# Sums of x in tiles of their own, no GpSimd work in the feed-forward stages until the norm, bias tables as tasks of the schedule

## The chip, the cores and the metric

The kernel runs on one core of one Trainium2 chip. The core has five engines with an instruction queue each, worked through in order: TensorE (PE, matmuls; its loads of weights are listed as PEld), VectorE (DVE), ScalarE (ACT), GpSimd (POOL) and SyncE (SP, which here issues most DMA transfers). Matmul results lie in eight banks of PSUM, named b0 to b7. An instruction that waits for another engine or for a transfer holds up all that is queued behind it on its engine. The metric is the device time of one execution in microseconds.

## The reference, cut

One layer of an encoder over 1024 prompt and 64 sample positions (1088 columns), width 1024, feed-forward width 2816, all in float32:

```python
def _swiglu(x, wi, wo):
    a, u = jnp.split(x @ wi, 2, axis=-1)
    return (jax.nn.silu(a) * u) @ wo

h = LN1(alpha*x + 0.5*SwiGLU1(x))
z = h @ w_in                        # all projections and gates
o_a = sparse attention (index, top 256 keys, T5 bias)
o_b = band attention (own chunk + 8 before, relative bias)
m = (sigmoid(g_a)*(o_a@w_branch_a) + sigmoid(g_b)*(o_b@w_branch_b)) @ w_out
h = LN2(alpha*h + m)
y = LN3(alpha*h + 0.5*SwiGLU2(h))
```

## The kernel before

**Precision.** A float32 product is made as three matmuls of a rounded type: each operand is split into a high part (a rounded copy) and a low part (the operand less its high part). A split so costs a copy ("hi") on ACT or DVE and a subtraction ("lo") on DVE or POOL. `factor` makes the split of a piece of the activations, `parts` inside `prepare` that of a 512-column piece of weights, in tiles w_s, of which there are two pairs (w_s0, w_s1).

**Stages.** The first feed-forward (0 to about 755 us), projections, attention and branches (to about 1760 us), the second feed-forward (to the end). Each feed-forward has a first stage (x @ wi, silu, product; about 500 us), a second stage of 63 items (h @ wo, about 200 us) and its last outputs with a layer norm. Nearly every traced instruction carries line 120 (L120), the helper `Timed.call` that records operations, so places in the program are named here by tiles.

**First stage.** The columns of the hidden layer are taken in 22 tiles f. From f=2 on, a tile's four block products are made by the scheme with seven products, in the order P2, P1, P6, P5, P3, P7, P4, of 48 matmuls each, with x cut in four blocks (two halves of rows, two of columns): A11, A12, A21, A22. P2 takes A12, P1 A11, P6 the sum S2 = S1 - A11, P5 S1 = A21 + A22, P3 S4 = A12 - S2 and P7 S3 = A11 - A21. `combos` makes these four sums from x (tiles y0 to y7, 128x544 halves), once, before and during f=2, one k of four at a time: sum on DVE or POOL, hi on ACT or DVE, lo on DVE or POOL, into tiles S1 to S4. The sums S1, S2, S4 are made in the tiles c1 and c2, S3 (`third`) in c0. c0, c1 and c2 (`G.t`) are also what every product uses: ACT copies the first product of a block from its banks (`c<-b`), which frees the banks for the next product, DVE adds the later ones to it (`c<-c,b`), silu and product run there, and 18 of the hidden tiles go from c by DMA to a buffer in DRAM (`ff_d<-c`).

**Second stage.** Each item is a product of 24 matmuls (about 3.0 us) of a factor of the kept hidden tiles with a sum of pieces of wo. The seven factors are again P2, P1, P6, P5, P3, P7, P4, nine items each: tiles a12, a11, a21, a22 are read from DRAM (`a<-ff_d`); sums of them (`a<-a,a`) are split into five tiles fac (`fac<-a`, `fac<-a,fac`). After a group of nine items DVE adds the eight banks to y (`y<-y,b`, eight instructions), and the next group's matmuls need those banks. The sums of pieces of wo were made during the first stage in tiles st (`sums_of_weights`, four sums per f on DVE from f=4 on: `st<-st,st`, loaded by `st<-in_wo_dram`) and put in DRAM.

**What sets the order.** A planner, class `Plan`, keeps queues of tasks and emulated clocks; it gives the next instruction to the queue whose turn its costs say it is. A task that may run on several engines (`shared`, `adders`, `w_h`, `x_h`) goes to the one that the emulated clocks say is free first, unless `st["solo"]` is true: then sums and lo parts go to DVE alone, hi parts to ACT alone. `solo` is set at the start of each feed-forward and cleared after seven of its steps (`SOLO`). The tables of bias for the attention (`bias_tables`: a load, a small matmul against `flip` or `btab` into bank 7, a copy on DVE, a store `bt_d<-one`, 16 times, DMAs on ACT's queue) run beside the first stage, stepped by a fixed rate of 0.3 steps per three matmuls.

Of the kernel before, what the change touches and what calls it, by code (L numbers as in the profile page):

```python
# [23 lines left out]
F32 = mybir.dt.float32  # L24
# [8 lines left out]
P = 128  # L33
# [297 lines left out]
def tile_trunk(ctx, tc, a):  # L331
# [520 lines left out]
    def combos(G, k):  # L852


        a11, a21, a12, a22 = (G.y[k + x][:, h * HT:(h + 1) * HT] for x in (0, 4) for h in range(2))
        s3, s1, s2 = (G.t[i].rearrange("p s c -> p (s c)") for i in range(3))

        def make(out, x, y, op, deps, reads):
            t = plan.task(shared(HT), "x_m", lambda e: of(e).tensor_tensor(out, x, y, op=op), deps, 2, None, reads)
            for i in (k, k + 4):  # L860
                G.read[i].append(t)
            return t

        def use(i, tasks):
            for s in range(2):
                G.user[i, s] = tasks

        def sums():
            m1 = make(s1, a21, a22, OP.add, G.used(1), [a21, a22])
            m2 = make(s2, s1, a11, OP.subtract, [m1] + G.used(2), [a11])  # L870
            t2 = factor(G, "S2", k, s2, [m2])
            m4 = make(s2, a12, s2, OP.subtract, [t2], [a12])
            use(1, [factor(G, "S1", k, s1, [m1]), m2])
            use(2, [factor(G, "S4", k, s2, [m4])])

        def third():
            m3 = make(s3, a11, a21, OP.subtract, G.used(0), [])
            use(0, [factor(G, "S3", k, s3, [m3])])
        return sums, third

    def add_ffn7(wi, wo, wl, G, gi, put, beside_it, last, end):
# [93 lines left out]
        def some():  # L975
            while G.hold and at.next < len(units):
                prepare()
# [202 lines left out]
        def sums_of_weights(j):  # L1180

            r = G.stage[j % 2]
            for i in range(4):
# [86 lines left out]
        def last_outputs():  # L1270
            fs = list(range(NF - 4, NF))
            wait(*(F[f].t[x, s] for f in fs for x in ("h1", "h2") for s in range(2)))
            last()
            some()
            us = [get_unit(f"l{d}", NF) for d in range(KT)]
# [89 lines left out]

        def normal():
            st["solo"] = False
        for i, j in enumerate(steps):
            if i == SOLO:
                jobs.append(normal)  # L1370
            jobs.append(j)
        jobs.append(last_outputs)
        jobs.append(end)

    HT, SUB = NT // 2, NT // 4
    EIGHT, SOLO = 2, 7
    SECONDS = (EIGHT + 1, NF - 1)
# [19 lines left out]
    def common(G):  # L1397
        G.xc, G.ready, G.user, G.read = {}, {}, {}, {d: [] for d in range(KT)}
        G.used = lambda i, s=None: [t for x in ((0, 1) if s is None else (s,)) for t in G.user.get((i, x), ())]
# [26 lines left out]
    def stage_tiles(G, name, side):  # L1426
        p = pool(open_(name), name, side)
        G.stage = [[p.tile([P, 512], F32, name=f"st{x}{i}") for i in range(4)] for x in range(2)]
        return p
# [13 lines left out]
    def make_ring1():  # L1443
        finish_streams()
        ring_tile(G1, "top1", None)
# [26 lines left out]
    def bias_tables():  # L1472


        one = G1.one
        row = one[:HEADS, :384]
        nc.scalar.dma_start(flip, a["flip"])
        yield
        for i in range(2):
            p = bank("ln")  # L1480
            kk = [(0, 32)] if i == 0 else [(0, 128), (128, 64)]
            for x, (k0, kn) in enumerate(kk):
                o = one[:, :384]
                nc.scalar.dma_start(o[:kn], a["hot_" + "ab"[i]][k0:k0 + kn])
                t = btab[:, x]
                nc.scalar.dma_start(t[:kn], a[("t5T", "relT")[i]][k0:k0 + kn])
                for _ in range(8):
                    yield
                nc.tensor.matmul(p[:HEADS, :384], t[:kn], o[:kn], start=x == 0, stop=x == len(kk) - 1)
                yield  # L1490
            nc.scalar.activation(row, p[:HEADS, :384], AF.Copy)
            for _ in range(2):
                yield
            nc.scalar.dma_start(row_d[i], row)
            for _ in range(8):
                yield
            for h in range(HEADS):
                t = one[:, :256]
                nc.scalar.dma_start(t, bass.AP(tensor=row_d[i].tensor, offset=row_d[i].offset + h * 384,
                                               ap=[[1, P], [1, 256]]))  # L1500
                for _ in range(8):
                    yield
                p = bank("ln")
                nc.tensor.matmul(p[:, :256], flip, t, start=True, stop=True)
                b = one[:, 256:]
                yield
                nc.vector.tensor_copy(b, p[:, :256])
                if i == 1:
                    nc.vector.tensor_scalar(b[:64, 192:], p[:64, 192:256], NEG, None, op0=OP.add)
                yield  # L1510
                nc.scalar.dma_start(bt_d[i][:, h * 256:(h + 1) * 256], b)
                yield

    def start_bias():
        beside(bias_tables(), 0.3)

# [1119 lines left out]
```

## Time and profile before

| | us |
|---|---|
| median of three runs | 2534.99 (2533.91 to 2536.92) |
| the profiled execution | 2534.35 |
| its span | 2532.5 |
| PE busy in it | 2438.6 (96%) |
| DVE, ACT, POOL busy | 1797.7 (71%), 1231.5 (49%), 477.1 (19%) |

The profile is one execution. A row of a timeline gives the start, the length in us, the engine, the tiles written and read, how many instructions are joined in the row, and in brackets how long the engine stood idle before it and what released it. The time of PE's instructions is modelled, so a stretch of the span is best weighed by how many matmuls it holds. PEclk is the mean granted clock of TensorE in a stretch, 1.00 being 2.4 GHz. In the view by stretches two columns follow it, the mean busy share of the DMA engines and what they moved in GB/s.

### The profile page before, as it was taken

To read this page: it belongs to the slowest core of one execution; us is meant where nothing else is said; L and a number is where in the kernel's file an instruction comes from. 1 tells how busy PE (TensorE), PEld (TensorE's weight loads), DVE (VectorE), ACT (ScalarE), POOL (GpSimd) and SP (SyncE) were. 2 spreads that over 40 slices of the span, in tenths; PEclk is the share of its full clock that TensorE was granted. 3 is DMA by queue.
4 is the path that set the end of the run, shared out by engine and by line. 5 is a ranking of instruction groups with operands and counts; after the bars stand their busy time and mean duration, and the time that the engine had idled before them with its cause. 6 is when DMAs were issued, how large, how long until landed. Compare 5 with 4: busy or idle time off the path is not lost.

```text
span 2532.5 us, 46846 instructions
## 1 busy us (share of the span) xinstructions
PE 2438.6 (96%) x17338; PEld 2382.9 (94%) x17338; DVE 1797.7 (71%) x4263; ACT 1231.5 (49%) x2611; POOL 477.1 (19%) x561
## 2 busy tenths in 40 slices
PE   9999999999999999999999999999989999999996
PEld 8999999999998899999999998998989999999995
DVE  6666655677776889898766767658866665668868
ACT  5333333322234598777857777524533333332224
POOL 0000000033233222122243332314000000003504
PEclk9999999999999999999999999999999999999997
DMA  5466533263222322322221112643246652245222
GB/s 182 120 191 195 174 103 90 78 202 112 84 81 94 117 75 77 96 81 82 71 79 59 56 39 69 191 145 116 77 126 191 192 156 90 64 138 189 84 72 71
DMA packets 221205, 285.42 MB, mean 113 GB/s; under 512 B 20704, under 2 KB 146512, under 8 KB 220944
## 3 DMA queue, kind: packets, MB, share of 16 engines
q1 hardware_dynamic: 200864, 257.40, 33.4%
q10 hardware_dynamic: 19552, 22.81, 2.8%
q8 instruction: 136, 2.23, 0.4%
q0 software_dynamic: 560, 2.21, 0.2%
q14 instruction: 93, 0.76, 0.1%
HBM read 207.62 MB, written 75.00 MB: 112 GB/s over the span
## 4 chain that ended last, share of the span: by engine, by line
PE 71%; DVE 11%; ACT 9%; issue 3%; DMA 3%; POOL 1%; ACTq 1%; SPq 0%; DVEq 0%; POOLq 0%
PE b L120 71%; ACT w L120 3%; ACT scores L120 2%; DVE w_s L120 2%; DVE y L120 1%; DVE w L120 1%; DVE k L120 1%; ACT pt L120 1%; DVE c L120 1%; DMA st<-in_wo_dram 1%; DVE pt L120 1%; ACT z L120 1%; DMA a<-ff_d 1%; DMA ff_d<-c 1%; ACTq L120 1%
## 5 line engine op out<-in xcount | busy, mean ns | idle before, releaser
L120 PE MATMUL b<-x,w_s 128*128 128x384 f32 (+1 forms) x3528 | 637.3, 332 | 4.7 <-ACT z L120 1.8
L120 PE MATMUL b<-A,w_s 128*128 128x272 f32 (+1 forms) x4824 | 633.9, 291 | 7.8 <-DVE y L120 3.4
L120 PEld LDWEIGHTS b<-A,w_s 128*128 128x128 f32 x4824 | 620.9, 190 | 12.1 <-ACT A L120 2.6
L120 PEld LDWEIGHTS b<-x,w_s 128*128 128x128 f32 x3528 | 587.5, 189 | 13.8 <-DVE x L120 2.4
L120 PE MATMUL b<-S,w_s 128*128 128x272 f32 x4032 | 520.4, 289 | 18.2 <-ACT c L120 18.2
L120 PEld LDWEIGHTS b<-S,w_s 128*128 128x128 f32 x4032 | 511.5, 189 | 22.2 <-ACT c L120 20.4
L120 ACT ACTIVATE w_s<-wr 128x512 fp32r<-128x512 f32 (+1 forms) x270 | 181.1, 671 | 368.5 <-PE b L120 223.1
L120 DVE TENSOR_TENSOR w_s<-wr,w_s 128x512 fp32r<-128x512 f32 (+1 forms) x323 | 247.4, 768 | 151.6 <-ACT w_s L120 142.3
L120 PE MATMUL b<-fac,w_s 128*128 128x272 f32 x1800 | 231.4, 290 | 4.4 <-DVE y L120 4.4
L120 PEld LDWEIGHTS b<-fac,w_s 128*128 128x128 f32 x1800 | 229.8, 190 | 4.9 <-issue 2.6
L120 POOL TENSOR_TENSOR w_s<-wr,w_s 128x256 fp32r<-128x256 f32 x196 | 149.8, 789 | 415.4 <-ACT w_s L120 169.9
L120 POOL TENSOR_TENSOR h<-c,h 128x272 fp32r<-128x272 f32 x2 | 1.5, 773 | 902.7 <-DVE h L120 902.7
L120 ACT ACTIVATE c<-b 128x272 f32<-128x272 f32 (+1 forms) x262 | 101.7, 391 | 104.7 <-PE b L120 90.2
L120 DVE TENSOR_TENSOR c<-c,b 128x272 f32<-128x272 f32 x240 | 103.5, 434 | 58.4 <-PE b L120 55.3
L120 DVE TENSOR_TENSOR pt<-b,pt 128x512 fp32r<-128x512 f32 (+4 forms) x184 | 96.5, 545 | 31.2 <-ACT pt L120 29.5
L120 ACT ACTIVATE fac<-a 128x544 fp32r<-128x544 f32 x75 | 49.4, 658 | 142.0 <-PE b L120 121.4
L120 PE MATMUL b<-pt,v 128*128 128x256 f32 (+3 forms) x672 | 103.6, 281 | 4.9 <-DVE pt L120 2.3
L120 PEld LDWEIGHTS b<-pt,v 128*128 128x128 f32 (+1 forms) x672 | 93.5, 188 | 13.6 <-DVE pt L120 4.5
L120 ACT ACTIVATE c<-c 128x272 f32<-128x272 f32 x160 | 68.7, 431 | 76.7 <-DVE c L120 73.8
L120 ACT ACTIVATE w<-w,mx 128x640 f32<-128x640 f32 (+5 forms) x144 | 100.5, 698 | 10.4 <-DVE mx L120 7.5
L120 ACT ACTIVATE w<-w,sm 128x640 f32<-128x640 f32 (+5 forms) x144 | 97.7, 697 | 9.7 <-DVE sm L120 4.6
L120 PE MATMUL b<-m,w_s 128*128 128x384 f32 (+1 forms) x576 | 99.7, 332 | 2.5 <-DVE w_s L120 1.4
(277 smaller groups left out, 3363.4 us busy)
## 6 DMA issues: line engine op xcount, KB each, us to landing
wr<-in_wi_dram SPq DMA_DIRECT2D x156, 256.0 KB, 3.1
ff_d<-c SPq DMA_DIRECT2D x144, 136.0 KB, 3.0
a<-ff_d SPq DMA_DIRECT2D x72, 272.0 KB, 3.7
st<-in_wo_dram SPq DMA_DIRECT2D x72, 256.0 KB, 5.3
tw_d<-st SPq DMA_DIRECT2D x72, 256.0 KB, 2.5
wr<-in_wz_dram SPq DMA_DIRECT2D x35, 512.0 KB, 3.7
wr<-tw_d SPq DMA_DIRECT2D x48, 256.0 KB, 2.7
q<-in_wi_dram SPq DMA_DIRECT2D x39, 256.0 KB, 3.1
```

The source lines that it names most:

```text
L120: r = real(*args, **kw)
```

## The change

Three edits. (1) `combos` makes the sums in the four tiles `G.stage[0]` (st00 to st03, now 544 wide; S1 in st0[k mod 2], S2 and S4 in st0[2 + k mod 2], S3 in st0[k mod 4]); who used one last is kept in `G.last`. The tiles c0, c1, c2 are no longer touched by it. (2) `solo` stays true through both stages and is cleared in `last_outputs`: until then all sums and lo parts go to DVE, all hi parts to ACT. That takes 41 POOL instructions from each feed-forward to DVE (30 `a<-a,a`, 11 lo parts) and, in each second stage, 47 hi copies of weights from DVE to ACT. (3) `bias_tables` yields an engine and an earliest time to the planner (`plan.chain`) instead of being stepped; `make_ring1` runs the planner until that chain is empty. Its last matmul stands at PE's instruction 3039 instead of 2970; the order of the other matmuls is the same.

```diff
@@ -853,7 +853,7 @@
         a11, a21, a12, a22 = (G.y[k + x][:, h * HT:(h + 1) * HT] for x in (0, 4) for h in range(2))
-        s3, s1, s2 = (G.t[i].rearrange("p s c -> p (s c)") for i in range(3))
+        s1, s2, s3 = (G.stage[0][i] for i in (k % 2, 2 + k % 2, k % 4))
         def make(out, x, y, op, deps, reads):
             t = plan.task(shared(HT), "x_m", lambda e: of(e).tensor_tensor(out, x, y, op=op), deps, 2, None, reads)
@@ -861,21 +861,20 @@
                 G.read[i].append(t)
             return t
-        def use(i, tasks):
-            for s in range(2):
-                G.user[i, s] = tasks
+        def last(x):
+            return G.last.get(x.tensor.name, [])
         def sums():
-            m1 = make(s1, a21, a22, OP.add, G.used(1), [a21, a22])
-            m2 = make(s2, s1, a11, OP.subtract, [m1] + G.used(2), [a11])
+            m1 = make(s1, a21, a22, OP.add, last(s1), [a21, a22])
+            m2 = make(s2, s1, a11, OP.subtract, [m1] + last(s2), [a11])
             t2 = factor(G, "S2", k, s2, [m2])
             m4 = make(s2, a12, s2, OP.subtract, [t2], [a12])
-            use(1, [factor(G, "S1", k, s1, [m1]), m2])
-            use(2, [factor(G, "S4", k, s2, [m4])])
+            G.last[s1.tensor.name] = [factor(G, "S1", k, s1, [m1]), m2]
+            G.last[s2.tensor.name] = [factor(G, "S4", k, s2, [m4])]
         def third():
-            m3 = make(s3, a11, a21, OP.subtract, G.used(0), [])
-            use(0, [factor(G, "S3", k, s3, [m3])])
+            m3 = make(s3, a11, a21, OP.subtract, last(s3), [])
+            G.last[s3.tensor.name] = [factor(G, "S3", k, s3, [m3])]
         return sums, third
     def add_ffn7(wi, wo, wl, G, gi, put, beside_it, last, end):
@@ -1179,7 +1178,7 @@
         def sums_of_weights(j):
-            r = G.stage[j % 2]
+            r = [x[:, :512] for x in G.stage[j % 2]]
             for i in range(4):
                 nc.sync.dma_start(r[i].rearrange("p (d c) -> p d c", d=4),
                                   wog[:, i % 2 * 4:i % 2 * 4 + 4, (2 * j + i // 2) * P:(2 * j + i // 2 + 1) * P])
@@ -1271,6 +1270,7 @@
             fs = list(range(NF - 4, NF))
             wait(*(F[f].t[x, s] for f in fs for x in ("h1", "h2") for s in range(2)))
             last()
+            st["solo"] = False
             some()
             us = [get_unit(f"l{d}", NF) for d in range(KT)]
             for b in range(3):
@@ -1363,17 +1363,12 @@
             want.append(((f"l{d}", NF), lambda q: q, wl[d // 2][:, d % 2 * 512:(d % 2 + 1) * 512]))
             unit(f"l{d}", NF)
-        def normal():
-            st["solo"] = False
-        for i, j in enumerate(steps):
-            if i == SOLO:
-                jobs.append(normal)
-            jobs.append(j)
+        jobs.extend(steps)
         jobs.append(last_outputs)
         jobs.append(end)
     HT, SUB = NT // 2, NT // 4
-    EIGHT, SOLO = 2, 7
+    EIGHT = 2
     SECONDS = (EIGHT + 1, NF - 1)
     SECOND, PAIRS = ("P2", "P1", "P6", "P5", "P3", "P7", "P4"), KEPT_OUT // 2
     NEEDS = dict(P2=("12",), P1=("11",), P6=("11", "21", "22"), P5=(), P3=(), P7=(), P4=())
@@ -1395,7 +1390,7 @@
                 G.xc["A21"] = G.xc[name]
     def common(G):
-        G.xc, G.ready, G.user, G.read = {}, {}, {}, {d: [] for d in range(KT)}
+        G.xc, G.ready, G.user, G.last, G.read = {}, {}, {}, {}, {d: [] for d in range(KT)}
         G.used = lambda i, s=None: [t for x in ((0, 1) if s is None else (s,)) for t in G.user.get((i, x), ())]
         G.sums_made = []
@@ -1425,7 +1420,7 @@
     def stage_tiles(G, name, side):
         p = pool(open_(name), name, side)
-        G.stage = [[p.tile([P, 512], F32, name=f"st{x}{i}") for i in range(4)] for x in range(2)]
+        G.stage = [[p.tile([P, n], F32, name=f"st{x}{i}") for i in range(4)] for x, n in enumerate((HT, 512))]
         return p
     def ring_tile(G, name, side):
@@ -1441,7 +1436,7 @@
     flip, btab = p1.tile([P, P], F32, name="flip"), p1.tile([P, 2, HEADS], F32, name="btab")
     def make_ring1():
-        finish_streams()
+        plan.until(lambda: not plan.busy("bias"))
         ring_tile(G1, "top1", None)
     G1.make_ring = make_ring1
@@ -1474,45 +1469,40 @@
         one = G1.one
         row = one[:HEADS, :384]
+        later = lambda e, t: (e, plan.t["pe"] + t)
+        yield "act"
         nc.scalar.dma_start(flip, a["flip"])
-        yield
         for i in range(2):
-            p = bank("ln")
             kk = [(0, 32)] if i == 0 else [(0, 128), (128, 64)]
             for x, (k0, kn) in enumerate(kk):
-                o = one[:, :384]
+                o, t = one[:, :384], btab[:, x]
+                yield "act"
                 nc.scalar.dma_start(o[:kn], a["hot_" + "ab"[i]][k0:k0 + kn])
-                t = btab[:, x]
                 nc.scalar.dma_start(t[:kn], a[("t5T", "relT")[i]][k0:k0 + kn])
-                for _ in range(8):
-                    yield
+                yield later("pe", 9000)
+                p = bank("ln") if x == 0 else p
                 nc.tensor.matmul(p[:HEADS, :384], t[:kn], o[:kn], start=x == 0, stop=x == len(kk) - 1)
-                yield
+                yield later("act", 1500)
             nc.scalar.activation(row, p[:HEADS, :384], AF.Copy)
-            for _ in range(2):
-                yield
+            yield later("act", 1000)
             nc.scalar.dma_start(row_d[i], row)
-            for _ in range(8):
-                yield
             for h in range(HEADS):
-                t = one[:, :256]
+                t, b = one[:, :256], one[:, 256:]
+                yield later("act", 4000)
                 nc.scalar.dma_start(t, bass.AP(tensor=row_d[i].tensor, offset=row_d[i].offset + h * 384,
                                                ap=[[1, P], [1, 256]]))
-                for _ in range(8):
-                    yield
+                yield later("pe", 9000)
                 p = bank("ln")
                 nc.tensor.matmul(p[:, :256], flip, t, start=True, stop=True)
-                b = one[:, 256:]
-                yield
+                yield "dve"
                 nc.vector.tensor_copy(b, p[:, :256])
                 if i == 1:
                     nc.vector.tensor_scalar(b[:64, 192:], p[:64, 192:256], NEG, None, op0=OP.add)
-                yield
+                yield later("act", 1500)
                 nc.scalar.dma_start(bt_d[i][:, h * 256:(h + 1) * 256], b)
-                yield
     def start_bias():
-        beside(bias_tables(), 0.3)
+        plan.chain("bias", bias_tables())
     def load_x(half, row, k):
         x = G1.y[4 * row + k][:, half * HT:(half + 1) * HT]
```

DVE's queue in the first feed-forward around the third sums of f=2 (y0 to y3 are halves of x, b2 and b3 banks, wr and q raw weights), before:

```order
L120 SCALAR_TENSOR_TENSOR c0_108<-c0_108,b2_590 128x272 [waits PE_49]
L120 SCALAR_TENSOR_TENSOR c0_108<-c0_108,b3_594 128x272 [waits PE_49,Activation_49]
L120 TENSOR_TENSOR c0_108<-y0_90 128x544 [waits DMAHW7_49,DMAHW6_49,DVE_49]
L120 TENSOR_TENSOR w_s1_130<-wr_111,w_s1_130 128x512 [waits DMAHW1_49,Activation_49]
L120 TENSOR_TENSOR q0_113<-wr_112,q0_113 128x512 [waits DMAHW2_49]
L120 TENSOR_TENSOR S3_106<-c0_108,S3_106 128x544 [waits Activation_49]
L120 TENSOR_TENSOR wr_112<-wr_112 128x512 [waits DMAHW5_49,DVE_49]
L120 TENSOR_TENSOR c0_108<-y1_91 128x544 [waits DVE_49]
L120 TENSOR_TENSOR wr_112<-wr_112,q0_113 128x512 [waits DVE_49]
L120 TENSOR_TENSOR wr_111<-wr_111,wr_112 128x512 [waits DVE_49]
L120 TENSOR_TENSOR S3_106<-c0_108,S3_106 128x544 [waits Activation_49]
```

and now:

```order
L120 SCALAR_TENSOR_TENSOR c0_108<-c0_108,b2_591 128x272 [waits PE_49]
L120 TENSOR_TENSOR st00_118<-y0_90 128x544
L120 TENSOR_TENSOR st01_119<-y1_91 128x544
L120 SCALAR_TENSOR_TENSOR c0_108<-c0_108,b3_596 128x272 [waits PE_49,Activation_49]
L120 TENSOR_TENSOR S3_106<-st00_118,S3_106 128x544 [waits Activation_49]
L120 TENSOR_TENSOR w_s1_130<-wr_111,w_s1_130 128x512 [waits DMAHW1_49,Activation_49]
L120 TENSOR_TENSOR S3_106<-st01_119,S3_106 128x544 [waits Activation_49]
L120 TENSOR_TENSOR st02_120<-y2_92 128x544
L120 TENSOR_TENSOR q0_113<-wr_112,q0_113 128x512 [waits DMAHW2_49]
L120 TENSOR_TENSOR st03_121<-y3_93 128x544
L120 TENSOR_TENSOR wr_112<-wr_112 128x512 [waits DMAHW5_49,DVE_49]
L120 TENSOR_TENSOR S3_106<-st02_120,S3_106 128x544 [waits Activation_49]
```

The sums no longer take turns on c0 and no longer wait for the DMAs that read it; two of them stand ahead of the last instruction on c0.

DVE's queue in the first feed-forward's second stage, ahead of the additions to y that end the third group (P2, P1 and then P6 is being prepared; a11, a21, a22 are kept hidden tiles), before, with the sums on POOL:

```order
L120 TENSOR_TENSOR fac3_5382<-a11_0_5352,fac3_5382 128x544 [waits Activation_49]
L120 CAST w_s1_130<-q1_114 128x512 [waits DMAHW5_49,PE_49]
L120 TENSOR_TENSOR w_s1_130<-q1_114,w_s1_130 128x512 [waits DVE_49,PE_49]
L120 TENSOR_TENSOR fac4_5383<-a11_1_5353,fac4_5383 128x544 [waits Activation_49]
L120 CAST w_s0_129<-wr_111 128x512 [waits DMAHW7_49,PE_49]
L120 TENSOR_TENSOR w_s0_129<-wr_111,w_s0_129 128x512 [waits DVE_49,PE_49]
L120 TENSOR_TENSOR fac0_5379<-a11_2_5354,fac0_5379 128x544 [waits Activation_49]
L120 CAST w_s0_129<-wr_112 128x512 [waits DMAHW1_49,PE_49]
L120 TENSOR_TENSOR w_s0_129<-wr_112,w_s0_129 128x512 [waits DVE_49,PE_49]
L120 TENSOR_TENSOR y0_90<-y0_90,b0_5744 128x272 [waits PE_49]
```

and now:

```order
L120 TENSOR_TENSOR a21_1_5362<-a21_1_5362,a22_1_5371 128x544 [waits DMAHW2_49,DMAHW0_49]
L120 TENSOR_TENSOR a11_1_5353<-a21_1_5362,a11_1_5353 128x544 [waits DVE_49]
L120 TENSOR_TENSOR w_s1_130<-q1_114,w_s1_130 128x512 [waits DMAHW5_49,PE_49,Activation_49]
L120 TENSOR_TENSOR fac4_5383<-a11_1_5353,fac4_5383 128x544 [waits Activation_49]
L120 TENSOR_TENSOR a21_2_5363<-a21_2_5363,a22_2_5372 128x544 [waits DMAHW5_49,DMAHW3_49]
L120 TENSOR_TENSOR a11_2_5354<-a21_2_5363,a11_2_5354 128x544 [waits DVE_49]
L120 TENSOR_TENSOR w_s0_129<-wr_111,w_s0_129 128x512 [waits DMAHW7_49,PE_49,Activation_49]
L120 TENSOR_TENSOR fac0_5379<-a11_2_5354,fac0_5379 128x544 [waits Activation_49]
L120 TENSOR_TENSOR a21_3_5364<-a21_3_5364,a22_3_5373 128x544 [waits DMAHW7_49,DMAHW0_49]
L120 TENSOR_TENSOR a11_3_5355<-a21_3_5364,a11_3_5355 128x544 [waits DVE_49]
L120 TENSOR_TENSOR y0_90<-y0_90,b0_5742 128x272 [waits PE_49]
```

The hi copies (CAST) have left the queue and the sums `a21<-a21,a22` and `a11<-a21,a11` have come in, the first of each pair with waits for two loads.

DVE's queue beside the tables of bias and the sums of weights, before at f=5:

```order
L120 COPY one_128<-b7_1895 128x256 [waits DMAHW6_49,PE_49]
L120 TENSOR_TENSOR w_s1_130<-wr_111,w_s1_130 128x512 [waits DMAHW3_49,PE_49,Activation_49]
L120 TENSOR_TENSOR c0_108<-c0_108,b2_1921 128x272 [waits PE_49]
L120 TENSOR_TENSOR st10_122<-st11_123,st10_122 128x512 [waits DMAHW2_49,DMAHW1_49]
L120 TENSOR_TENSOR c0_108<-c0_108,b3_1939 128x272 [waits PE_49,Activation_49]
```

and now at f=5:

```order
L120 TENSOR_TENSOR c0_108<-c0_108,b2_1446 128x272 [waits PE_49]
L120 COPY one_128<-b7_1475 128x256 [waits DMAHW2_49,PE_49]
L120 TENSOR_TENSOR st10_122<-st11_123,st10_122 128x512 [waits DMAHW3_49,DMAHW2_49]
L120 TENSOR_TENSOR c0_108<-c0_108,b3_1463 128x272 [waits PE_49,Activation_49]
L120 TENSOR_TENSOR w_s1_130<-wr_111,w_s1_130 128x512 [waits Activation_49]
```

In both the copy to `one` and a sum of st that waits for loads stand ahead of c0 + b3.

## Rows read from the trace of the kernel before

**Rows 1.** PE's waits by releaser, whole span: us, times, longest:

```profile
PE b L120 <- ACT c L120: 19.6, 10, 6.3
PE b L120 <- DVE y L120: 7.8, 4, 2.4
```

**Rows 2.** Timeline of PE, the first feed-forward's P6 at f=2:

```profile
75.63 14.35 PE L120 MATMUL b<-S,w_s 128*128 128x272 f32 x96 [4.22 <-ACT c L120]
```

**Rows 3.** Timelines of DVE and ACT ahead of that:

```profile
60.49 0.78 DVE L120 SCALAR_TENSOR_TENSOR c<-c,b 128x272 f32<-128x272 f32 x2
63.28 0.73 DVE L120 TENSOR_TENSOR c<-y 128x544 f32<-128x544 f32 x1 [2.01 <-DMA ff_d<-c]
...
75.18 0.69 ACT L120 ACTIVATE c<-b 128x272 f32<-128x272 f32 x2 [1.18 <-DVE S L120]
```

**Rows 4.** Stretches: length, busy (instructions) of PE, PEld, DVE, ACT, POOL; PEclk:

```profile
520.00:540.00 20.00, 20.00 (x161) 20.00 (x161) 12.09 (x22) 4.62 (x7) 0.79 (x1) 1.00 0.70 230
70.00:80.00 10.00, 5.78 (x31) 5.56 (x30) 5.21 (x10) 3.81 (x8) 0.00 (x0) 0.67 0.32 106
1830.00:1850.00 20.00, 13.75 (x100) 13.53 (x99) 14.25 (x24) 7.98 (x16) 0.00 (x0) 0.83 0.20 65
560.00:580.00 20.00, 17.63 (x129) 17.44 (x128) 17.52 (x25) 5.25 (x9) 11.45 (x8) 0.91 0.58 186
```

**Rows 5.** Timelines of PE and DVE, the second feed-forward's P6:

```profile
1842.02 13.54 PE L120 MATMUL b<-S,w_s 128*128 128x272 f32 x96 [6.25 <-ACT c L120]
...
1829.67 0.73 DVE L120 TENSOR_TENSOR c<-y 128x544 f32<-128x544 f32 x1 [2.89 <-DMA ff_d<-c]
...
1835.36 1.29 DVE L120 TENSOR_TENSOR w_s<-wr,w_s 128x512 fp32r<-128x512 f32 x2
```

**Rows 6.** Timeline of PE, three stretches of the second stages:

```profile
512.61 55.96 PE L120 MATMUL b<-fac,w_s 128*128 128x272 f32 x432 [2.05 <-DVE y L120]
570.95 4.39 PE L120 MATMUL b<-fac,w_s 128*128 128x272 f32 x21 [2.37 <-DVE y L120]
...
2317.26 2.98 PE L120 MATMUL b<-A,w_s 128*128 128x272 f32 x22 [1.42 <-DVE y L120]
```

**Rows 7.** Timelines of DVE and POOL, the first feed-forward's second stage:

```profile
510.55 1.45 DVE L120 TENSOR_TENSOR fac<-a,fac 128x544 fp32r<-128x544 f32 x1 [1.34 <-ACT fac L120]
...
550.48 0.71 DVE L120 TENSOR_TENSOR fac<-a,fac 128x544 fp32r<-128x544 f32 x1
...
554.56 1.89 DVE L120 TENSOR_TENSOR fac<-a,fac 128x544 fp32r<-128x544 f32 x1
...
554.08 10.17 POOL L120 TENSOR_TENSOR a<-a,a 128x544 f32<-128x544 f32 x6 [4.08 <-DMA a<-ff_d]
```

**Rows 8.** DVE from 500 to 700 us by operation: us, mean ns, idle before:

```profile
L120 DVE TENSOR_TENSOR fac<-a,fac 128x544 fp32r<-128x544 f32 x54 | 48.7, 902 | 1.7 <-ACT fac L120 1.7
...
L120 DVE CAST w_s<-wr 128x512 fp32r<-128x512 f32 x35 | 21.6, 617 | 22.0 <-PE b L120 22.0
```

**Rows 9.** POOL by operation, 0 to 800 us and 1700 us to the end:

```profile
L120 POOL TENSOR_TENSOR a<-a,a 128x544 f32<-128x544 f32 x30 | 47.2, 1597 | 13.5 <-DMA a<-ff_d 13.2
...
L120 POOL TENSOR_TENSOR a<-a,a 128x544 f32<-128x544 f32 x30 | 47.3, 1602 | 12.9 <-DMA a<-ff_d 12.5
```

**Rows 10.** Timelines of PE, ACT and DVE beside the tables of bias:

```profile
165.89 6.28 PE L120 MATMUL b<-S,w_s 128*128 128x272 f32 x48 [1.06 <-ACT c L120]
186.74 5.88 PE L120 MATMUL b<-S,w_s 128*128 128x272 f32 x45 [2.13 <-ACT c L120]
...
257.63 6.25 PE L120 MATMUL b<-S,w_s 128*128 128x272 f32 x48 [1.28 <-ACT c L120]
...
277.82 2.14 PE L120 MATMUL b<-S,w_s 128*128 128x272 f32 x15 [0.99 <-ACT c L120]
...
165.44 0.40 ACT L120 ACTIVATE c<-b 128x272 f32<-128x272 f32 x1 [2.71 <-DVE one L120]
...
184.90 0.69 DVE L120 TENSOR_TENSOR st<-st,st 128x512 f32<-128x512 f32 x1 [4.31 <-DMA st<-in_wo_dram]
```

## The prediction

> **What bounds the kernel now.** TensorE is busy for 96% of the span, so the time is its instructions plus the places where it stands idle, and none of its matmuls is removed or added. I read its list of waits by releaser first [rows 1]: what can be won by freeing other engines stands there. The two largest entries are ACT's copies out of the banks (19.6 us, ten times) and DVE's additions to y (7.8 us, four times). The other entries belong to attention and norms, which the change leaves alone. Then the timeline of TensorE gave the place of each wait, and the view by stretches what it really cost: an undisturbed stretch of 20 us holds 161 matmuls at full clock, 0.124 us each [rows 4]; what a disturbed stretch holds less, times that, is its loss, the slower clock after the pause included.
>
> **Edit 1, the sums in tiles of their own.** In the first feed-forward P6 of f=2 starts 4.22 us late, released by an ACT copy to c [rows 2]. That copy was itself held by DVE's low part of S3: c0 served all four third sums in turn, each waiting for the split of the one before, and the first for the DMA that reads c0 (2.01 us) [rows 3]. P1's last product is out at 71.41 (75.63 less 4.22), and its banks come free only after 75.18. The stretch from 70 to 80 us holds 31 matmuls instead of 80.5, at a mean granted clock of 0.67: 49.5 x 0.124 = 6.1 us lost [rows 4].
>
> In the new order the sums wait neither for that DMA nor for one another, so c0 is free for ACT as soon as its DMA has read it, about 63.3. What is late next? P6's weights. From 60.49 on DVE has, ahead of P6's first low part, two instructions on 272 columns (0.4 us each), eight on 544 (an instruction of 0.72 us follows the one before it after 0.64) and five on 512 (0.6): 0.8 + 5.1 + 3.0 = 8.9 us, plus 0.6 for the low part itself. That is 70.0; the second low part is out about 71.0. Both lie before 71.41. So I take all 6.1, with 0 to 6.1 as bounds.
>
> The second feed-forward shows the same picture, 6.25 us [rows 5]; its 20 us from 1830 on hold 100 matmuls instead of 161: 61 x 0.124 = 7.6 us [rows 4]. TensorE is due at 1835.77 there (1842.02 less 6.25), and P6's first low weights were written at 1835.36 to 1836.6 even before. In the new queue DVE has lost the 2.89 us wait and gets to them earlier by it, but has four more instructions ahead of them (4 x 0.64 = 2.6). So they come about 1835.7; up to 0.9 us of pause can remain. I take 7.3. Together edit 1 gives **13.4**.
>
> **Edit 2 in the second stages.** Three waits for DVE's y there: 2.05, 2.37 and 1.42 us [rows 6]. What makes DVE late is POOL's company: the same low part of fac takes 0.71 us alone and 1.89 us while POOL runs sums [rows 7], 0.902 in the mean over 54; the casts take 0.617 over 35 [rows 8]. POOL's sums take 1.6 us each [rows 9].
>
> Price of the move, for the first feed-forward's second stage: on DVE come 39 of the 41 instructions at 0.72 us alone, +28 us. Off DVE go 47 casts (21.6 us for 35 of them [rows 8], some 28 for all). The slowing goes too, (0.902 - 0.71) x 54 = 10 us on fac alone, and about as much on the other forms. Net, DVE wins 10 to 30 us of 200. None of that is time by itself; it counts only where y is late.
>
> At 570.95 the additions start at 570.38 behind a fac of 1.89 and a low part of 1.63 us. Preparing P6, an item now has two sums, a low part of weights and one of fac on DVE: 4 x 0.64 = 2.6 of the 3.0 us that TensorE takes. DVE keeps pace and is there about 567, before the 568.58 (570.95 less 2.37) at which TensorE runs out. So that pause goes: 560 to 580 us holds 129 instead of 161, which is 32 x 0.124 = 4.0 us. The pause at 2317 goes likewise, 1.4 (no clock loss in it). At 512.61 the additions stand behind a fac low part that waits for its hi part, which waits for a load; only its length shrinks from 1.45 to 0.72: 0.7. Sum **6.1**, bounds 0 and 7.8.
>
> A rule of the skill can be weighed here. The row shows a DVE subtraction at 1.89 beside POOL's 1.6 and at 0.71 alone [rows 7, 9]. The Trainium skill (SBUF — State Buffer, "Who interferes with whom") says that DVE instructions with two inputs in SBUF contend with GpSimd instructions that read SBUF, and calls the shared pair of ports an exclusive lock. By that rule each of the 39 POOL instructions would keep DVE out for its own length, and moving them would win DVE up to 39 x (1.6 - 0.72) = 34 us; by the rows' slowing it is 10 to 30. The trace agrees in kind (0.71 becomes 1.89), and the sum above doesn't change, since DVE needs only about 2 us at each y.
>
> **What the move costs elsewhere.** ACT gets the 47 hi copies, at 0.63 against DVE's 0.42 us. It was busy for a quarter of that stage, and weights are split an item or more ahead in two pairs of tiles, so the cover is about 3 us. Bounds 0 and 47 x 0.2 = 9 us each, taken near the lower end as the cover is large: **1** for both feed-forwards. DVE now waits in its own queue for loads of a: POOL's waits for them were 13.2 and 12.5 us [rows 9]. The third pair was there at 554.08 [rows 7], and DVE asks for the first from about 556, so I take 0.5 for both.
>
> **Edit 3, tables of bias.** Five waits between 165 and 278 us lie near the tables and the sums of weights. Three are the tables' (165.89 the first, 257.63 the last of three, 3.24 us in all): ACT's queue holds a DMA that waits for DVE's copy to `one` or for another transfer, 2.71 us in the row, and TensorE waits behind it. In the new order these DMAs mostly stand where ACT's next urgent copy is 9 us away. Two (2.13 and 0.99, together 3.12) are another matter: DVE waits 4.31 us for a load of st ahead of c0 + b3 [rows 10]. That order stands at two places in the new queue too, at other f. So I count the first three, less some 0.7 us where a table's DMA still stands between two copies: **2.5**, bounds -1 (both inversions last longer, as each carries a table's copy as well) and +5.5.
>
> **The sum.** 13.4 + 6.1 + 2.5 - 1.5 = 20.5 us, against the profiled execution: 2534.35 - 20.5 = 2513.9, **2514** us. That execution lies 0.6 us below the median of the runs shown, so the median may be 0.6 higher; that is below what I can resolve.
>
> **Rivals.**
> - *Only edit 1 works (the second stages and the tables give nothing).* DVE is still late at y, as loads hold it in front of the additions, and the tables' waits move on to other copies. For it: the loads of a end most of POOL's waits, and DVE inherits them; two inversions remain. Against it: the items leave 0.4 us of slack each. 2534.35 - 13.4 + 1.5 = about 2522.
> - *The change doesn't do what it says: the weights take the place of the sums.* If each of DVE's 16 extra or moved instructions ahead of P6's weights costs 0.1 us more than counted, the weights are 1.6 us late twice, and the pause keeps its slow clock: half of edit 1 is lost. With 2 us from the rest missing too: 2527. For it: the weights at 1836 are barely in time even now [rows 5].
> - *Slower.* DVE takes over POOL's waits for loads whole, ahead of the additions to y. This decides from the point where loads are issued so late that DVE waits for them at every pair; then 13.2 + 12.5 = 25.7 us go on DVE, the gain of edit 2 is lost, and the time is 2534.35 - 13.4 - 2.5 + 25.7 = 2544. Against it: the loads were there some 2 us before DVE would ask.
> - *More.* The clock stays up in further places, all five waits of edit 3 go and the full 2.05 at 512: another 7 us, 2507.
>
> **How the numbers follow.** My forecast 0.6 (2509 to 2519 by its own bounds), only edit 1 0.16, the weights late 0.12, more 0.07, slower 0.05. The range leaves out the slower case and the tails: 2506 to 2526. About 0.2%, 5 us, is what a measurement of this kernel tells from no change. Faster takes all but the slower case and the worst tail of the weights' case: 0.90; same 0.06; slower 0.04.
>
> **What would show it.** Right: TensorE's waits for ACT c fall from 19.6 to about 4 us, those for y from 7.8 to about 3; P6 of f=2 follows P1 without a gap in both feed-forwards; the low parts of fac take 0.72 us everywhere; POOL has no row between the start and the last outputs. Wrong: TensorE waits for DVE w_s at P6 (second rival), or DVE shows long waits for a<-ff_d ahead of y (third), or the waits between 165 and 280 us stand as before at other tiles (first).

## The result

The changed kernel takes 2506.05 us in the median of four runs (2503.94 to 2507.51), the one before 2535.95 in the runs beside it: ratio 0.9881, interval 0.9865 to 0.9897. A second set of runs gave 0.9897 (0.9883 to 0.9911). That is 26 to 30 us less, where 20.5 were forecast. The way and the places were right; the size was a quarter to a half more than forecast, and the median lies at the lower end of my range (2506), with the ratio just outside it. The traced execution took 2507.51 us, its span 2505.7.

TensorE's waits by releaser in the changed kernel (us in total, times, longest), against [rows 1]:

```profile
PE b L120 <- ACT c L120: 4.4, 7, 1.3
PE b L120 <- DVE y L120: 2.8, 2, 1.8
```

The forecast was 4 and 3. P6 of f=2 starts without a wait in the first and the second feed-forward (timeline of PE, against [rows 2, 5]; the 96 matmuls of the row are P6, P5, P3 and P7, 24 each):

```profile
70.33 12.14 PE L120 MATMUL b<-S,w_s 128*128 128x272 f32 x96
...
1817.50 12.13 PE L120 MATMUL b<-S,w_s 128*128 128x272 f32 x96
```

The two weights' low parts that I put at 70.0 and 71.0 are written in DVE's timeline 3 to 4 us before TensorE needs them at 70.33:

```profile
65.85 0.68 DVE L120 TENSOR_TENSOR w_s<-wr,w_s 128x512 fp32r<-128x512 f32 x1
...
66.80 0.68 DVE L120 TENSOR_TENSOR w_s<-q,w_s 128x512 fp32r<-128x512 f32 x1
```

In the second stage DVE's rows have their undisturbed length, and it hardly waits for the loads it took over (DVE from 488 to 690 us by operation, against [rows 8]; us, mean ns, idle before):

```profile
L120 DVE TENSOR_TENSOR fac<-a,fac 128x544 fp32r<-128x544 f32 x63 | 45.4, 722 | 48.5 <-ACT fac L120 48.5
...
L120 DVE TENSOR_TENSOR a<-a,a 128x544 f32<-128x544 f32 x36 | 25.6, 720 | 0.9 <-DMA a<-ff_d 0.7
```

TensorE passes the places of the pauses at 570.95 and 2317.26 [rows 6] without a wait; the pauses at the start of the two second stages are left (timeline of PE; the matmul that waited at 2317.26 stands in the row from 2281.05 on):

```profile
498.65 190.07 PE L120 MATMUL b<-fac,w_s 128*128 128x272 f32 x1512 [0.95 <-DVE y L120]
...
2235.79 12.28 PE L120 MATMUL b<-A,w_s 128*128 128x272 f32 x96 [1.82 <-DVE y L120]
...
2281.05 12.22 PE L120 MATMUL b<-A,w_s 128*128 128x272 f32 x96
```

Matching the two traces at the same matmuls gives where the 26.8 us between the spans came from. The lead is how much earlier a matmul starts in the changed kernel; a line of the table is what the lead grows by (in the first from 0.9 us at 35 us to 7.5 at 90; times are those of the trace of before):

| stretch | forecast | measured |
|---|---|---|
| P6 of f=2, first feed-forward | 6.1 | 6.6 |
| tables and sums of weights, 130 to 310 us | 2.5 | 5.8 |
| second stage, first feed-forward | 4.7 | 6.7 |
| P6 of f=2, second feed-forward | 7.3 | 7.8 |
| second stage, second feed-forward | 1.4 | 3.3 |
| all else (start +0.9, the rest given back) | -1.5 | -3.4 |

Of the last line 1.4 us are lost between 755 and 1790 us and 2.0 in the second feed-forward's first stage behind P6. In the second trace of the changed kernel (e4) it is 0.8 and 0.1, so most of it differs from one execution to the next; that none of it is a cost of the moved work is not shown.

### The profile page after: what moved, and what is told of

Read it like the earlier page. It is cut to its first block, busy times and chain, and to the rows that moved or that the text cites. A ratio compares the mean times of both kernels' runs of the same rounds, so it can differ in the third digit from the quotient of the medians.

```text
span 2505.7 us, 46746 instructions
## 1 busy us (share of the span) xinstructions
PE 2432.4 (97%) x17338; PEld 2379.4 (95%) x17338; DVE 1752.6 (70%) x4246; ACT 1285.1 (51%) x2712; POOL 349.0 (14%) x477
## 4 chain that ended last, share of the span: by engine, by line
PE 76%; DVE 9%; ACT 8%; issue 3%; DMA 3%; POOL 1%; ACTq 0%; SPq 0%; DVEq 0%; POOLq 0%
PE b L120 76%; ACT w L120 2%; ACT scores L120 2%; DVE w L120 1%; DVE y L120 1%; DVE k L120 1%; ACT pt L120 1%; DMA g<-g_d 1%; DVE pt L120 1%; DVE scores L120 1%; DVE w_s L120 1%; ACT z L120 1%; DVE sc L120 0%; ACTq L120 0%; DMA st<-in_wo_dram 0%
## 5 line engine op out<-in xcount | busy, mean ns | idle before, releaser
L120 ACT ACTIVATE w_s<-wr 128x512 fp32r<-128x512 f32 (+1 forms) x345 | 227.4, 660 | 383.0 <-PE b L120 207.1
L120 DVE TENSOR_TENSOR w_s<-wr,w_s 128x512 fp32r<-128x512 f32 (+1 forms) x323 | 229.9, 714 | 143.8 <-ACT w_s L120 139.3
L120 POOL TENSOR_TENSOR lns<-lns,lnq 128x384 f32<-128x384 f32 (+1 forms) x25 | 27.1, 1084 | 739.2 <-ACT lnq L120 738.1
L120 POOL TENSOR_TENSOR y<-y,c 128x384 f32<-128x384 f32 (+1 forms) x15 | 17.3, 1174 | 706.0 <-DVE acc L120 691.3
L120 PEld LDWEIGHTS b<-pt,v 128*128 128x128 f32 (+1 forms) x672 | 93.5, 188 | 13.5 <-DVE pt L120 4.3
```

The source lines that it names most:

```text
L120: r = real(*args, **kw)
```

## The experiments

**The three edits apart.** e1 to e3 apply one edit each to the kernel before (its parts of the diff above, nothing else); e4 is the changed kernel again. Gains are told by the ratios, which compare runs made beside each other; the medians give 13, 11 and 3 us for e1 to e3, and 28 for e4.

> The kernel before with edit 1 alone (sums of x in tiles of their own). Theory by the terms of the sum: P6 of f=2 follows P1 without a gap in both feed-forwards, 6.6 us in the first and 7 us in the second, so 13 to 14 us less than before (ratio 0.9945). Rival, the weights take the place of the sums: TensorE waits for w_s there, half of it is lost, 6 to 7 us less (0.9975). The other waits (165 to 278 us, the additions to y) should stand as before; if those between 165 and 278 us shrink here, the st tiles and not the tables were their cause.

Measured: 2520.99 us, ratio 0.9956 (0.9944 to 0.9969), 11 us less. P6 starts without a wait in both feed-forwards (6.6 and 7.8 us in the trace); nothing waits for its weights. The five waits between 165 and 278 us stand, the second 0.7 us shorter than before (1.15, 1.41, 0.92, 1.23, 0.75), so the st tiles' second use is not their cause.

> The kernel before with edit 2 alone (no GpSimd work until the last outputs). Theory: DVE's low parts of fac fall from 0.90 to 0.72 us in the mean, the pauses of 2.37 and 1.42 us for y go and so do the slow-clock stretches behind the pauses at 512 and 2260 us; 9 to 10 us less than before (0.9963). Rival, the slow clock there was an accident of one execution: 7 us less or fewer (0.9972). Rival, DVE inherits GpSimd's waits for the loads of a: no gain, and rows of DVE waiting for a<-ff_d of 10 us and more.

Measured: 2523.06 us, 0.9964 (0.9951 to 0.9976), 9 us less, as the theory said. DVE waits 0.2 us ahead of the sums of a in the first feed-forward's second stage.

> The kernel before with edit 3 alone (tables of bias as tasks). Theory after the result: all five waits between 165 and 278 us shrink, also the two that I put down to loads of st, since a table's copy no longer shifts the loads and additions around them; 5 to 6 us less than before (0.9978). Rival, my prediction's split: only the three of the tables go, 2.5 to 3.3 us less (0.9988), and two pauses of 1 to 2 us behind loads of st remain at other f.

Measured: 2530.61 us, 0.9994 (0.9984 to 1.0004): 1 to 2 us less, within the noise, and yet in its trace all five waits are gone but one of 0.18, and the lead grows by 6.9 us between 128 and 310 us. The trace also shows where some of it went: the additions to y, still in GpSimd's company, came later than in the trace of before (timeline of PE; [rows 6] has 1.42 us for it):

```profile
2308.77 4.59 PE L120 MATMUL b<-A,w_s 128*128 128x272 f32 x24 [3.50 <-DVE y L120]
```

The same place cost 2.36 in e1. The 1.42 of one trace was thus the lowest of three, and my term for it too small. That this is all that hides edit 3's gain in e3 is not shown.

> The changed kernel once more, for a second trace of it and for a ratio beside the three parts on the same chip. If the three parts add up, its gain is the sum of theirs: 13.5 + 9.7 + 5.8 = 29 us (0.9886); if parts overlap (a gain of one hides behind another's wait), it is less than their sum. In the stages that the change leaves alone (755 to 1760 us) the two traces of it should show how far one execution differs from the next: the first trace lost some 3 us there against before.

Measured: 2505.87 us, 0.9897 (0.9883 to 0.9911). The three ratios multiply to 0.9914; the difference is within the intervals, so neither overlap nor more than the sum is shown.

**Edit 3 undone.**

> The changed kernel with edit 3 undone (tables of bias stepped at the old fixed rate; edits 1 and 2 stay). Edit 3 alone took five waits out of the trace between 165 and 278 us (a gain of 6.9 us there), but its runs were only 1 to 3 us below before, with a spread of 10 us. Theory: the gain is real and was drowned by the varying waits for y that GpSimd's company causes; with edit 2 in, undoing edit 3 costs 5 to 7 us (about 2511.5), with a spread of some 5 us. Rival: edit 3 is worth only 1 to 3 us, what is won there being lost further on (about 2508).

Measured: 2511.91 us, 0.9909 (0.9892 to 0.9926), 6 us over e4 by the medians and 3 by the ratios; its trace loses 6.1 us against e4's between 130 and 310 us, with five waits of 0.60 to 1.83 us.

**Edit 2 in halves.** e6 gives the sums in the second stages to GpSimd, e12 lets DVE have the hi copies of weights again:

```diff
-                return plan.task(shared(HT), "x_m", ...)
+                return plan.task((("pool", 146 + 2.1 * HT),), "x_m", ...)
```

```diff
-                t1 = task((("act", ...), ("dve", ...))[alone], "w_h", ...)
+                t1 = task((("act", ...), ("dve", ...))[slice(0, 2) if u.kind[0] == "x" else alone], "w_h", ...)
```

> The changed kernel with one part of edit 2 undone: in the second stages the sums of a (36 in each feed-forward) go to GpSimd alone; hi copies stay on ACT, lo parts on DVE. Theory, company of GpSimd slows DVE and makes y late: the mean of fac's low part rises from 0.72 to 0.85 us and more, TensorE waits for y at the P6 additions again (1 to 3.5 us each, different in each execution), 5 to 9 us more than the changed kernel, and the spread of the runs grows. Rival, the moved hi copies were what freed DVE: under 2 us more.

Measured: 2525.45 us, 0.9966 (0.9952 to 0.9979), 17 us more than e4 by the ratios and 20 by the medians, and more than edit 2 alone gains (e2). The direction is that of the theory, the size about twice its upper end; the runs did not spread more (4 us). TensorE's longest wait in the first feed-forward's second stage, and DVE's rows before it (timelines of PE and DVE, then DVE from 490 to 590 us and GpSimd from 480 to 760 us by operation):

```profile
585.28 1.02 PE L120 MATMUL b<-fac,w_s 128*128 128x272 f32 x3 [5.31 <-DVE y L120]
...
568.31 0.72 DVE L120 TENSOR_TENSOR fac<-a,fac 128x544 fp32r<-128x544 f32 x1 [3.75 <-ACT fac L120]
...
574.03 5.49 DVE L120 TENSOR_TENSOR fac<-a,fac 128x544 fp32r<-128x544 f32 x3
...
584.71 0.42 DVE L120 TENSOR_TENSOR y<-y,b 128x272 f32<-128x272 f32 x1
...
L120 DVE TENSOR_TENSOR fac<-a,fac 128x544 fp32r<-128x544 f32 x31 | 33.9, 1099 | 20.7 <-ACT fac L120 20.7
...
L120 POOL TENSOR_TENSOR a<-a,a 128x544 f32<-128x544 f32 x36 | 59.8, 1683 | 543.1 <-DMA a<-ff_d 539.4 <-DVE fac L120 2.2 <-DVE w_s L120 0.7
```

Three low parts take 5.49 us instead of 2.0, and the first addition to y starts at 584.71, when TensorE has stood for 5 us. The addition itself, with one input in PSUM, keeps its 0.42. The place is another than in the kernel before: here the additions that end P6 are late, there those that end P1 (570.38). And company is not all that e6 shows: at 568.31 DVE has stood for 3.75 us, for a hi copy on ACT that itself waited 4.26 us for a GpSimd sum. While P6 is prepared, GpSimd needs 2 x 1.68 us for the two sums of an item, TensorE 3.0 us for the item. What reading beside DVE costs by itself is left to e7 and e8.

> The changed kernel with the other part of edit 2 undone: in the second stages the hi copies of weights may again go to DVE or ACT, whichever the planner says is free first (67 of them go back to DVE in both together); all sums and low parts stay on DVE, nothing on GpSimd. With e6 it splits edit 2. Theory, company was the cost and not the copies: a copy takes 0.34 us of DVE start to start, an item then fills some 2.9 of TensorE's 3.0 us where sums are made and far less elsewhere; the same time as the changed kernel within 2 us (2506), no waits for y at the P6 additions. Rival, DVE had no room left and the copies matter too: waits for y or for w_s come up, 3 to 8 us more.

Measured: 2505.74 us, 0.9885 (0.9866 to 0.9904): the same as e4. DVE does 39 hi copies of weights at 0.427 us in the first feed-forward's stage, fac's low parts still take 0.719, and no addition at P6 is late. The copies were not what mattered.

**The company itself.** e7 and e8 add to the changed kernel work on GpSimd that nobody uses, in the first feed-forward's second stage (the two edits in one, without the making of the tile `G.beside`):

```diff
+            if G is G1:
+                t = G.beside
+                nc.gpsimd._real.tensor_tensor(t[:, 1], t[:, 0], t[:, 0], op=OP.add)    # e7 alone
+                nc.gpsimd._real.memset(t, 0.0)                                         # e8 alone
+                nc.gpsimd._real.memset(t[:, 0], 0.0)                                   # e8 alone
```

> The changed kernel with 63 idle additions on GpSimd (two inputs in SBUF, 128x544, nobody uses the result) put into the first feed-forward's second stage, one after the other from its start, about 100 us. It measures the disputed cost by itself. If GpSimd's reads keep DVE out: fac's and w_s's low parts take 1.6 to 1.9 us there (3.5 us an item against TensorE's 3.0), 10 to 30 us longer in all, and nothing changes in the second feed-forward. Rival, the slow DVE rows of before came from loads arriving at that time: rows of 0.72 us, no longer than the changed kernel.

> The same with GpSimd fills in place of the additions (126 fills of 1088 and 544 columns, about 95 us of GpSimd that writes SBUF and reads nothing). The Trainium skill (SBUF, 'Who interferes with whom') says that a two-input DVE instruction contends only with GpSimd's reads: DVE rows of 0.72 us as in the changed kernel and its time, against 10 to 30 us more if any GpSimd work slows DVE.

Measured: e7 2534.24 us, 28 more than e4; e8 2506.58, the same (one run each). DVE from 490 to 590 us and GpSimd by operation, e7:

```profile
L120 DVE TENSOR_TENSOR fac<-a,fac 128x544 fp32r<-128x544 f32 x25 | 33.2, 1331 | 3.0 <-ACT fac L120 3.0
...
L120 DVE TENSOR_TENSOR y<-y,b 128x272 f32<-128x272 f32 x12 | 4.5, 426 | 0.0
...
L1248 POOL TENSOR_TENSOR beside<-beside 128x544 f32<-128x544 f32 x63 | 86.9, 1379 | 4.9
```

and e8:

```profile
L120 DVE TENSOR_TENSOR fac<-a,fac 128x544 fp32r<-128x544 f32 x34 | 24.5, 723 | 23.5 <-ACT fac L120 23.5
...
L1248 POOL MEMSET beside<- 128x1088 f32 x63 | 63.9, 1014 | 3.6
```

GpSimd is busy for 92 us (87 and its gaps) in the one and 99 in the other; where it reads, DVE's low parts nearly double and TensorE waits up to 13.5 us for y, where it only writes, nothing changes. It is the reading, not loads that arrive at that time: both kernels have the same loads. The Trainium skill (SBUF — State Buffer, "Who interferes with whom") states this difference; the two runs agree with it, 1331 against 723 ns.

**What edit 3 did.** e9 and e10 give the sums of pieces of wo an earliest time, in the changed kernel and in e5:

```diff
-                last = [plan.task(shared(512), "w_x", go, last, 6, None, [r[x], r[y]])]
+                last = [plan.task(shared(512), "w_x", go, last, 6, None, [r[x], r[y]], plan.t["pe"] + 6000.0)]
```

> The changed kernel with one edit more: the sums of pieces of wo (st) get an earliest time 6 us after their loads are issued, so on DVE's queue none that waits for a load stands ahead of c0 + b3 any more (two places in the changed kernel). Theory, that order is what is left of the waits between 100 and 300 us: the waits of 0.2 to 1.0 us there go, 1 to 2 us less than the changed kernel (2504). Rival, the waits only move behind other copies: the same time and as many short waits.

Measured: 2505.55 us, 0.9876 (0.9859 to 0.9892). The waits between 100 and 300 us are gone from the trace; its trace gains 2.0 us more there than e4's, which is below what the runs resolve.

> The changed kernel with edit 3 undone (e5) and the sums of pieces of wo delayed by the same 6 us: both old orders of st ahead of c0 + b3 are gone while the tables keep their fixed rate. This splits edit 3's gain of 6 us. My prediction's split: the two waits behind loads of st (1.83 and 0.60 us in e5) go, the three beside the tables (0.75, 0.96, 0.87) stay: 2.5 to 3 us less than e5 (2509). Rival, all five hang on the tables' rate: as many and as long waits as in e5, 2512. Rival, all five hang on st: 5 to 6 us less, 2506.

Measured: 2506.29 us, 0.9883 (0.9869 to 0.9898), 5.6 us less than e5: the third case, which I had thought least of. One wait of the five is left in e10 (timeline of PE):

```profile
157.86 6.28 PE L120 MATMUL b<-S,w_s 128*128 128x272 f32 x48 [1.19 <-ACT c L120]
```

So four of five hang on DVE's waits for loads of st, also two of the three that [rows 10] show behind a table's DMA. For the fifth no run shows it, but the order is the same there: in e10 the copy to `one` at 156.59 us stands behind three sums of st, the first of which waited 0.94 us for a load. The chain at one of the places in e5, timelines of DVE, ACT and PE:

```profile
243.90 0.69 DVE L120 TENSOR_TENSOR st<-st,st 128x512 f32<-128x512 f32 x1 [1.22 <-DMA st<-in_wo_dram]
...
245.57 0.69 DVE L120 TENSOR_TENSOR st<-st,st 128x512 f32<-128x512 f32 x1 [0.37 <-DMA st<-in_wo_dram]
246.18 0.42 DVE L120 COPY one<-b 128x256 f32<-128x256 f32 x1
...
246.62 0.33 ACTq L120 DMA_DIRECT2D bt_d<-one  x1
247.05 0.63 ACT L120 ACTIVATE w_s<-wr 128x512 fp32r<-128x512 f32 x1 [2.55 <-DVE one L120]
...
248.02 1.76 PE L120 MATMUL b<-S,w_s 128*128 128x272 f32 x12 [0.96 <-ACT c L120]
```

A load holds DVE; behind it stands the copy to `one`; ACT's queue holds the store of `one`; behind that stand ACT's copies, and TensorE waits for the bank. The tables were the middle of the chain, not its head. It is cut by moving the tables (edit 3) or the sums (e10), and as far as the runs resolve, one is as good as both (e9).

**How far it goes.** e11 leaves out the clearing of `solo` in `last_outputs`.

> The changed kernel with solo never cleared: from the last outputs of the first feed-forward on through projections and attention the planner gives no sum or low part to GpSimd either (145 GpSimd instructions fewer). It tests how far the lesson goes. Theory: DVE is busy for eight tenths and more of most slices there, and GpSimd's 150 us of low parts become 70 us of DVE; where DVE is the one that TensorE waits for, that costs more than the company did: 5 to 20 us more than the changed kernel. Rival, company is dearer than the work also here: faster than 2500.

Measured: 2505.72 us (2501.80 to 2509.86), 0.9882 (0.9864 to 0.9900): the same time as the changed kernel, which neither the theory nor the rival had. GpSimd is busy for 238.5 us instead of 349, DVE for 1777.6 instead of 1752.6, and the waits change owners: TensorE's wait for DVE's sums of the norms rises from 3.1 (e4) to 12.7 us, those for GpSimd's norms (5.4) vanish.

## Why the prediction was right in kind, and which steps failed

Three terms of the sum of 20.5 failed: edit 3 (2.5, measured 5.8 us), the second stages (6.1, measured 10.0) and the costs (1.5, none found). Edit 1 was 1.0 too small. Together that is 9.7 us, of which 3.4 are lost again elsewhere.

**Edit 1** was right in place, mechanism and size (13.4 forecast, 14.4 in the trace). DVE was even earlier at P6's weights than I worked out, since it starts the third sums earlier and nothing holds the queue; the residual of 0.3 did not come. The second rival (weights take the place of the sums) has no row: e1 shows no wait for w_s at P6. Its time was wrong besides: half of 13.4 and 2 us more give 2522.6 by its own terms, not 2527.

**Edit 2** was right in its mechanism: e7 and e8 show GpSimd's reads as the cause, e6 and e12 that the sums and not the copies carry it. What the moved low parts give by themselves no run separates. DVE's busy time in the stage falls by 19 us (144.3 us in 190 from 510 on, 125.6 in 190 from 495), inside my 10 to 30. Only the size of what TensorE gets from it was off, 10.0 for 6.1. The terms that were mis-sized are the pauses at 512 and at 2260: I priced the first at 0.7 and the second at nothing, by their lengths alone, though the sum for P6 and 570 had counted matmuls. Measured they are 2.6 and 1.7, since in the trace of before the clock falls behind both, and in that of the changed kernel it stays up. Stretches of 5 us behind the wait at the second feed-forward's first y, and behind that at 512.61 (before, after each):

```profile
2259.86:2264.86 5.00, 5.00 (x28) 5.00 (x29) 1.68 (x3) 0.87 (x3) 0.35 (x1) 0.66 0.48 161
```

```profile
2235.79:2240.79 5.00, 5.00 (x40) 5.00 (x41) 2.77 (x5) 1.02 (x3) 0.00 (x0) 1.00 0.48 159
```

```profile
512.61:517.61 5.00, 5.00 (x28) 5.00 (x29) 2.14 (x4) 0.45 (x2) 0.60 (x1) 0.66 0.49 160
```

```profile
498.65:503.65 5.00, 5.00 (x40) 5.00 (x41) 3.18 (x6) 1.41 (x3) 0.00 (x0) 1.00 0.42 139
```

28 matmuls against 40 are 12 x 0.124 = 1.5 us, at 2260 on top of a pause of nearly the same length (1.99 and 1.82), at 512 on top of one that shrinks from 2.05 to 0.95. Two such stretches are 3.0 of the 3.9 us that I missed. They are not shown to be edit 2's work. Without edit 2 the clock stays up too: behind 512's place in e1 and e3, after pauses of 1.30 and 1.60 us, and behind 2260's in e3, after 2.19 us (the stretch below). In e1 it falls at 2260's, after 1.94 us, and with edit 2 it falls there in e9 and e10, after 1.82 and 1.91 us. So how much of the 3.0 us is edit 2's work and how much is luck of the two executions compared stays open; by the runs e2 gains 9 us (6 to 12 by its interval), which fits either.

```profile
2250.81:2255.81 5.00, 5.00 (x40) 5.00 (x41) 2.37 (x4) 1.04 (x3) 0.37 (x1) 1.00 0.48 160
```

**Edit 3** was mis-sized, 5.8 for 2.5, because its step was wrong: I split five waits into three of the tables and two of the sums of weights, and counted only the first. e10 shows that four of them, two of either kind, go when the sums of weights wait. The [rows 10] that I read as two kinds, ACT behind DVE's `one` and DVE behind a load, were two links of one chain; the row that joins them, DVE's copy to `one` behind a sum that waits, I did not look at. The two places that I feared in the new queue do appear (133.47 and 199.55 us, waits of 0.23 and 0.98), at a smaller price. The part ahead of the prediction puts both order rows at f=5; that of before is the one at 184.90 us, two tiles later.

**The costs I subtracted** (hi copies on ACT 1, loads on DVE 0.5) did not come: every stretch of 20 us in the changed kernel's second stages behind their first pause holds 161 or 162 matmuls. The slower rival fell with them: DVE waits 0.7 us for loads in that stage instead of GpSimd's 13.2 [rows 9].

**The range** was too narrow below. What came is nearly the rival *more* (2507, chance 0.07): all five waits of edit 3 went and the clock stayed up in further places, though of the 2.05 us at 512 only 1.1 went. That edit 3's five waits could go together had a reason, the chain, which I did not see, and so its chance was too small. A pause's price in one trace differs between executions besides: at the additions that P6 waits for in the first feed-forward, the traces with GpSimd's sums show 2.37 (before), 3.54 (e1) and 2.55 (e3).

**Slips ahead of the prediction** that change no term of the sum: a product of the first stage has 24 matmuls, not 48, and P1 comes before P2; the additions to y shown before P6 end the second group (P1), not the third; and 42 GpSimd instructions, not 41, leave each feed-forward (30 sums, 12 low parts).

## What to carry to other kernels

Follow a wait past its first releaser to the head of the chain: three engines' waits at four of five places had one cause, a load that was waited for too early in an in-order queue. Price a pause by the matmuls that the stretch behind it holds, not by its length, and by more than one trace. And before sharing elementwise work between DVE and GpSimd, compare the length of DVE's rows beside GpSimd's reading instructions with their length alone: in these second stages the helper cost more than it carried, while it was free where it only wrote; in the stages between, leaving it out changed nothing (e11).

## What the runs showed of the hardware

- A DVE instruction with two inputs in SBUF goes from 0.72 to 1.8 or 1.9 us beside a GpSimd addition (before, e6), one with an input in PSUM stays (0.426 us, e7), and beside GpSimd fills nothing slows (0.723, e8). A DVE copy, with one input in SBUF, did slow beside GpSimd's sums (1.5 us for 0.42 in the trace of before).
- TensorE's clock after pauses of much the same length is not the same each time. After the wait of 1.82 us in the changed kernel it stayed at 2.4 GHz, and after one of 2.19 us at the same place in e3 too; after one of 1.82 us there in e9 the next 5 us hold 28 matmuls at a mean granted clock of 0.66, between the two levels:

```profile
2234.16:2239.16 5.00, 5.00 (x28) 5.00 (x28) 2.08 (x4) 0.49 (x2) 0.00 (x0) 0.66 0.49 158
```

What else decides it the runs leave open.
